# A compression weight tile in a spent chunk of the recurrence's table, and 32x32 products on two strips of columns

## The chip, the cores and the metric

The kernel runs on one core of one Trainium2 chip. The metric is the device time of one launch in microseconds (us); lower is better. The kernel before takes 841.3 us (median of 3 runs, 841.02 to 841.45).

## The reference, cut to what matters

One decoder block for 512 tokens of width 1024 in float32: a norm, one input projection (`w_in`), two mixers, gates, an output projection, and a gated MLP. The change touches the two mixers.

The attention mixer compresses its keys and values before it uses them: blocks of 32 tokens with stride 16 are flattened to 2048 numbers and go through a two-layer MLP with GELU.

```python
flat = blocks.transpose(0, 1, 3, 2, 4).reshape(b, n_cmp, g, CMP_BLOCK * dh)
return jax.nn.gelu(flat @ w1) @ w2          # w1: 2048 x 256, one for keys, one for values
```

The RWKV-7 mixer is a recurrence over tokens, for 8 heads of size 64:

```python
sa = jnp.einsum('bhij,bhj->bhi', state, a_t)
state = state * w_t[:, :, None, :] + sa[..., None] * b_t[:, :, None, :] + v_t[..., None] * k_t[:, :, None, :]
return state, jnp.einsum('bhij,bhj->bhi', state, r_t)
```

## The kernel before, in words

**Products.** Weights come in tiles of 512 KB. For most, ScalarE rounds the tile `raw` to `whi`, VectorE (sometimes GpSimd) makes the rest `wlo`, and TensorE multiplies the activations, likewise in two parts `hh` and `hl`, by both: 16 products with `whi`, 8 with `wlo` (`dense_fm_g`). A new tile is asked for by `wnext`: it issues the load of a tile further on (`wload`, L262 to L268), splits the next one (`wsplit_`), and hands out the one that is due. `raw` has three buffers (L266), `whi` and `wlo` two each. All these loads are issued by SyncE (SP), whose queue is in order: a load that waits holds up those behind it. The order of the loads is that of the generator `weight_tiles` (L215 to L256).

**Compression weights.** The first layer's weights come in four tiles for keys and four for values, (0,k), (0,v) to (3,k), (3,v), 512 rows each. They are used unsplit (`eng` is `None`), straight from `raw`, so a raw buffer is held until TensorE has read it. Between them stand gate tiles, called G1, G2, G3 and so on here: (0,k), (0,v), (1,k), (1,v), G1, (2,k), (2,v), G2, (3,k), (3,v), G3, G4, ...

**The recurrence** works on 8 chunks of 64 tokens. Its 64x64 tables for all chunks, head pairs and two halves are in `AB` (128 partitions x 8 chunks x 1024). Before the chunk loop, a lower triangle in each table is inverted. Its 32x32 diagonal blocks are inverted by VectorE (`Nn`, `Tn`, L618 to L633) and written back by transposes (L730, L735). The 32x32 block below the diagonal needs two products per table: `below` (L740) makes the first and puts it in `Y1`, `left` (L749) the second and puts it in `AB`. Each call does 16 tables for the two groups g (partitions 0 to 63 and 64 to 127) and evicts by ScalarE, one instruction per group:

```python
mm(ptr[g][half(g, 1), 32 * i:32 * i + 32], ABq[g][half(g, 0), q0 + i, 32:64], Y1[half(g, 0), q0 + i], ...)
act(Y1[half(g, 1), q0:q0 + 16].rearrange("p q s -> p (q s)"), ptr[g][half(g, 1)])
```

`half(g, b)` are partitions 64g + 32b to 64g + 32b + 31. TensorE's array is addressed by the partitions of the operands (strips of rows) and of the output (strips of columns). The inverse's block runs in TensorE's written order (L760 to L768): gate tile 0, `below(0)`, `below(16)`, a part of the key/value projection (`kv_proj`), `left(0)`, another part, `left(16)`, another part.

**The chunk loop** (L931 to L993), again in TensorE's written order, does for chunk c: products of the old state (`M`, `AR`), `Xs` copied out by VectorE, products `AB` x `Xs` and `AB` x `UV` of the next chunk, `UV` copied out by ScalarE (one half, L956) and VectorE (other half, L957), products of `UV` with `BKT` (new state) and with `AB` (output), and every second chunk a group norm on VectorE and ScalarE. Between these steps the generator `fill_chain` (L880) puts other TensorE work: the rest of the key/value projection, the compression (`compress`, L786), one pair of tiles at a time with 16 passes each, and gate tiles. The compression's input table `Rk` lies in `sg1` and is written by VectorE (L126, L790); it shares that memory with `Y1`. After pair 3 comes GELU on ScalarE and VectorE. ScalarE's and VectorE's own orders come from a scheduler.

**After the loop's chunk 3** the first half of `AB` is used again, for the bias rows `BT` (L907, loaded in chunks 4 and 5), and the second half for gates.

Of the kernel before, what the change touches and what calls it, by code (L numbers as in the profile page):

```python
# [10 lines left out]
F32 = mybir.dt.float32  # L11
# [69 lines left out]
def hybrid_block(ctx: ExitStack, tc: tile.TileContext, A: dict, out: bass.AP):  # L81
# [15 lines left out]
    wp = ctx.enter_context(tc.tile_pool(name="w", bufs=1))  # L97
# [12 lines left out]
    def mmb():  # L110
        return bank("mm", 4)

    def pa():
        return bank("a", 2)

    def pb():
        return bank("b", 2)

    def mm(o, l, r, start, stop):
        te.matmul(o, lhsT=l, rhs=r, start=start, stop=stop)  # L120

    def act(o, i, f=AF.Copy, **kw):
        sc.activation(o, i, f, **kw)  # L123
# [32 lines left out]
    for name in ("rwkv_mu", "rwkv_w0", "rwkv_a0", "rwkv_k_k", "rwkv_k_a", "rwkv_r_k", "rwkv_ln_g", "rwkv_ln_b"):  # L156
        r0, n = ROWS[name]
# [57 lines left out]
    def weight_tiles():  # L215
        def cols(w, o, kt=KT, eng=v):
            return w[:, o:o + 128], kt, 128, eng

        def rows(w, o, n, kt=KT, eng=v):
            step = 1024 // n  # L220
            for i, k0 in enumerate(range(0, kt, step)):
                kn = min(step, kt - k0)
                yield w[128 * k0:128 * (k0 + kn), o:o + n], kn, n, eng[i] if type(eng) is list else eng

        pool_ = nc.gpsimd
        yield cols(w_in, O_RWKV + 1536, eng=pool_)
        yield cols(w_in, O_RWKV + 1664, eng=pool_)
        for p in range(NH2):
            for o in (512, 0, 1024):
                yield cols(w_in, O_RWKV + o + 128 * p)  # L230
        yield cols(w_in, O_KC)
        yield from rows(w_in, O_Q, 512, eng=[v, pool_, ("spare", pool_), v])
        yield cols(w_in, O_VC)
        yield from rows(w_in, O_KS, 256, eng=[v, ("spare", v)])
        for m in range(NGA):
            yield cols(w_in, O_GA + 128 * m)
        yield from rows(w_in, O_KW, 280, eng=pool_)
        for m in range(NGA, KT):
            if m < 4:
                for s4 in range(m if m > NGA else 0, m + 1):  # L240
                    for s_ in "kv":
                        yield A["cmp_w1_" + s_][0][512 * s4:512 * s4 + 512], 4, 256, None
            yield cols(w_in, O_GA + 128 * m)
        for m in range(NGB):
            yield cols(w_in, O_GB + 128 * m)
        for m in range(KT):
            if m + NGB < KT:
                yield cols(w_in, O_GB + 128 * (m + NGB), eng=pool_ if m else v)
            yield cols(A["w_proj_b"][0], 128 * m, NH2, eng=pool_)
        for m in range(KT):  # L250
            yield cols(A["w_proj_a"][0], 128 * m, NH2)
        yield from rows(A["w_out"][0], 0, 512)
        yield from rows(A["w_out"][0], 512, 512, eng=())
        for f in range(NF):
            yield cols(A["w_up"][0], DFF + 128 * f)
            yield cols(A["w_up"][0], 128 * f)  # L256
        for hf in range(2):
            yield from rows(A["w_down"][0], 512 * hf, 512, NF)

    wtiles = weight_tiles()  # L260
    loads, ahead, late = [], [], []
    def wload():  # L262
        nxt = next(wtiles, None)
        if nxt is not None:
            src, kt, n, eng = nxt
            raw = wp.tile([128, kt, n], F32, name="raw", tag="raw", bufs=3)  # L266
            nc.sync.dma_start(raw, src.rearrange("(k p) n -> p k n", p=128))
            loads.append((raw, kt, n, eng))  # L268

# [29 lines left out]
    def wnext(kt, n):  # L299
        wload()  # L300
        if loads and loads[0][3] != ():
            wsplit()
        w = ahead.pop(0)
        assert list((w if type(w) is not tuple else w[0]).shape) == [128, kt, n]
        return w
# [3 lines left out]
    _, hs = norm_tiles(xp)  # L309
    ssx = xp.tile([128, NT], F32, name="ssx")  # L310
    wload()
    wload()
    wload()

# [16 lines left out]
    with tc.manual_schedule(engines={getattr(mybir.EngineType, e) for e in ("PE", "Activation", "DVE", "Pool")}):  # L331
# [20 lines left out]
        raw = loads.pop(0)[0]  # L352
# [73 lines left out]
    AB = abp.tile([128, NCH, NH2, 2, 128], F32, name="AB")  # L426
# [190 lines left out]
    ABq = [AB.rearrange("p c a r t -> p (c a) r t")[:, :, g, :] for g in range(2)]  # L617
# [4 lines left out]
    for g in range(2):  # L622
        for b in range(2):
            r = 64 * g + 32 * b
            v.transpose(Nn[r:r + 32].rearrange("p t s -> p t s"),
                        ABq[g][r:r + 32, :, 32 * b:32 * b + 32].rearrange("p q t -> p t q"))
    for k in range(31):
        m, n = 31 - k, k + 1
# [99 lines left out]
    Y1 = sg1[:, 1:3].rearrange("p m s -> p (m s)").rearrange("p (q s) -> p q s", q=32)  # L728
# [3 lines left out]
    for b in (1, 0):  # L732
        for g in range(2):
            r = 64 * g + 32 * b
            v.transpose(ABq[g][r:r + 32, :, 32 * b:32 * b + 32].rearrange("p q t -> p t q"), Tn[r:r + 32])  # L735

    def half(g, b):
        return slice(64 * g + 32 * b, 64 * g + 32 * b + 32)

    def below(q0):  # L740
        ptr = [pa(), pb()]
        for i in range(16):
            for g in range(2):
                mm(ptr[g][half(g, 1), 32 * i:32 * i + 32], ABq[g][half(g, 0), q0 + i, 32:64], Y1[half(g, 0), q0 + i],
                   True, True)
        for g in range(2):
            act(Y1[half(g, 1), q0:q0 + 16].rearrange("p q s -> p (q s)"), ptr[g][half(g, 1)])

    def left(q0):  # L749
        ptr = [pa(), pb()]  # L750
        for i in range(16):
            for g in range(2):
                mm(ptr[g][half(g, 0), 32 * i:32 * i + 32], Y1[half(g, 1), q0 + i], ABq[g][half(g, 1), q0 + i, 32:64],
                   True, True)
        for g in range(2):
            act(ABq[g][half(g, 0), q0:q0 + 16, 32:64], ptr[g][half(g, 0)].rearrange("p (q t) -> p q t", t=32))

    fill = kv_proj(1, 280)
    urgent.clear()
    with tc.manual_schedule(engines={mybir.EngineType.PE, mybir.EngineType.Pool}):  # L760
        for m in range(NGA):
            act(siga[m], dense_fm(hh, hl))
        below(0)
        below(16)
        next(fill)
        left(0)
        next(fill)
        left(16)  # L768
        next(fill)
        norm_keys(0)  # L770
        rstd(qss.rearrange("p t h -> p (t h)"), DH)
        for t in range(NT):
            nc.gpsimd.tensor_tensor(heads(qn[:, t]), heads(qn[:, t]), qss[:, t, :, None].to_broadcast([128, 8, DH]),
                                    op=ALU.mult)
# [505 lines left out]
    for i in range(KT // 2):  # L1280
        raw = loads.pop(0)[0]
# [9 lines left out]
    with tc.manual_schedule(engines=KTS):  # L1291
        for t in range(NT):
            qs = slice(128 * t, 128 * t + 128)
            p = mmb()
# [52 lines left out]
    for hf in range(2):  # L1347
        bo = dense_tok(512, aT[:, 0], aT[:, 1], NF)
        for t in range(NT):
            n = 256 if hf and t == NT - 1 else 512  # L1350
# [32 lines left out]
```

## Time and profile before

| | |
|---|---|
| median of 3 runs | 841.3 us (841.02 to 841.45) |
| profiled execution | 841.33 us |
| its span, first to last instruction | 839.5 us |
| TensorE products busy | 824.8 us, 98% |
| VectorE busy | 514.1 us, 61% |
| ScalarE busy | 405.4 us, 48% |
| GpSimd busy | 52.4 us, 6% |
| granted TensorE clock | 1.0 throughout |

All times in views are us from the start of the span. PE is TensorE (PEld its weight loads), DVE VectorE, ACT ScalarE, POOL GpSimd, SPq the issue of a DMA by SyncE. A row of a timeline is: start, length, engine, line of the kernel, operation, tile written <- tiles read, shape, count, and in brackets the engine's idle time before it with what ended it. The profile takes a float32 product as two passes, so 32 products show as x64. Nearly all products and evictions go through helpers, so they carry the lines L120 (product), L123 (ScalarE), L126 and L135 (VectorE); they are told apart by their tiles. `sg` stands for `sg0` and `sg1`, which `Y1` and `Rk` lie in, and `QK` for the buffer of GELU's operands among others.

### The profile page before, as it was taken

To read this page: it belongs to the slowest core of one execution; us is meant where nothing else is said; L and a number is where in the kernel's file an instruction comes from. 1 tells how busy PE (TensorE), PEld (TensorE's weight loads), DVE (VectorE), ACT (ScalarE), POOL (GpSimd) and SP (SyncE) were. 2 spreads that over 40 slices of the span, in tenths; PEclk is the share of its full clock that TensorE was granted. 3 is DMA by queue.
4 is the path that set the end of the run, shared out by engine and by line. 5 is a ranking of instruction groups with operands and counts; after the bars stand their busy time and mean duration, and the time that the engine had idled before them with its cause. 6 is when DMAs were issued, how large, how long until landed. Compare 5 with 4: busy or idle time off the path is not lost.

```text
span 839.5 us, 12845 instructions
## 1 busy us (share of the span) xinstructions
PE 824.8 (98%) x5097; PEld 669.9 (80%) x5097; DVE 514.1 (61%) x998; ACT 405.4 (48%) x784; POOL 52.4 (6%) x69
## 2 busy tenths in 40 slices
PE   7999999999999999999999999999999999999998
PEld 6777778887677876777788988888888888888886
DVE  5478779964556678888665566665555666322222
ACT  6766654452555767677343454444444444221210
POOL 5200020140000100111000000000000000000000
PEclk9999999999999999999999999999999999999999
DMA  7432222335462320000266033333333332233421
GB/s 229 113 80 72 76 76 77 83 102 168 128 126 62 84 57 13 26 26 26 63 222 206 1 101 100 94 90 93 101 101 101 100 96 89 92 101 113 138 75 51
DMA packets 109104, 78.73 MB, mean 94 GB/s; under 512 B 3869, under 2 KB 97748, under 8 KB 109044
## 3 DMA queue, kind: packets, MB, share of 16 engines
q1 hardware_dynamic: 106512, 73.51, 29.7%
q10 hardware_dynamic: 1060, 2.55, 1.0%
q0 software_dynamic: 1472, 1.86, 1.0%
q8 instruction: 40, 0.66, 0.3%
q14 instruction: 20, 0.16, 0.1%
HBM read 74.56 MB, written 2.29 MB: 92 GB/s over the span
## 4 chain that ended last, share of the span: by engine, by line
PE 53%; DVE 0%; DVEq 0%; issue 0%
PE ps_mm L120 52%; PE ps_b L203 0%; PE ps_a L203 0%; PE ps_a L120 0%; PE ps_b L1187 0%; PE ps_mm L1187 0%; DVE x L126 0%; DVEq L1379 0%; PE ps_a L1139 0%
## 5 line engine op out<-in xcount | busy, mean ns | idle before, releaser
L296 DVE TENSOR_TENSOR wlo<-raw,whi 128x1024 fp32r<-128x1024 f32 (+1 forms) x111 | 131.5, 1186 | 186.5 <-PE ps_mm L120 157.8
L120 PE MATMUL ps_mm<-hh,whi 128*128 128x512 f32 (+1 forms) x624 | 242.6, 391 | 0.7 <-ACT whi L123 0.7
L120 PE MATMUL ps_mm<-hl,whi 128*128 128x512 f32 (+1 forms) x624 | 240.4, 387 | 0.0
L123 ACT ACTIVATE whi<-raw 128x1024 fp32r<-128x1024 f32 (+3 forms) x124 | 123.3, 996 | 170.9 <-PE ps_mm L120 141.6
L120 PE MATMUL ps_mm<-hh,wlo 128*128 128x512 f32 (+1 forms) x624 | 151.7, 384 | 0.0
L120 PEld LDWEIGHTS ps_mm<-hh,whi 128*128 128x128 f32 x624 | 117.3, 188 | 27.5 <-ACT whi L123 1.1
L120 PEld LDWEIGHTS ps_mm<-hl,whi 128*128 128x128 f32 x624 | 117.4, 188 | 23.4 <-issue 1.0
L120 PEld LDWEIGHTS ps_mm<-hh,wlo 128*128 128x128 f32 x624 | 115.1, 188 | 23.3
L120 PE MATMUL ps_mm<-whi,aT 128*128 128x512 f32 x352 | 84.5, 390 | 0.0
L120 PEld LDWEIGHTS ps_mm<-whi,aT 128*128 128x128 f32 x352 | 65.9, 188 | 14.3 <-issue 0.4
L135 DVE SCALAR_TENSOR_TENSOR cgv<-ps_mm,cw,cgv 128x511 f32<-128x511 f32 (+1 forms) x88 | 65.4, 746 | 1.6
L123 ACT ACTIVATE cgv<-ps_mm,cw 128x512 f32<-128x512 f32 x44 | 34.3, 781 | 23.3 <-PE ps_mm L120 23.3
L120 PE MATMUL ps_mm<-wlo,aT 128*128 128x512 f32 x176 | 44.3, 389 | 0.0
L123 ACT ACTIVATE P<-P,nm 128x512 f32<-128x512 f32 (+3 forms) x64 | 35.4, 553 | 14.9 <-DVE nm L1161 14.9
L123 ACT ACTIVATE aT<-cgv 128x512 fp32r<-128x512 f32 x22 | 13.9, 632 | 56.8 <-DVE cgv L126 56.8
L120 PEld LDWEIGHTS ps_mm<-wlo,aT 128*128 128x128 f32 x176 | 33.0, 188 | 6.9
L123 ACT ACTIVATE cgv<-cgv 128x512 f32<-128x512 f32 x22 | 13.9, 632 | 41.0 <-DVE cgv L135 41.0
L296 POOL TENSOR_TENSOR wlo<-raw,whi 128x512 fp32r<-128x512 f32 (+3 forms) x13 | 20.4, 1569 | 204.3 <-PE ps_mm L120 148.5
L1161 DVE CUSTOM_DVE_ANT_0 P<-ps_a,AB 128x512 f32<-128x512 f32 (+3 forms) x64 | 29.4, 483 | 4.2 <-PE ps_a L120 3.7
L126 DVE TENSOR_TENSOR x<-x,ps_mm 128x512 f32<-128x512 f32 (+1 forms) x17 | 11.0, 654 | 23.0 <-PE ps_mm L120 21.2
L126 DVE TENSOR_TENSOR aT<-cgv,aT 128x512 fp32r<-128x512 f32 x22 | 15.2, 693 | 14.7 <-ACT aT L123 14.7
L120 PE MATMUL ps_a<-KH,qst 128*128 128x512 f32 (+3 forms) x64 | 21.3, 348 | 1.6 <-DVE nm L1161 0.9
(356 smaller groups left out, 1203.4 us busy)
## 6 DMA issues: line engine op xcount, KB each, us to landing
raw<-in_w_up_dram SPq DMA_DIRECT2D x44, 512.0 KB, 3.7
raw<-in_w_in_dram SPq DMA_DIRECT2D x38, 512.0 KB, 3.8
raw<-in_w_down_dram SPq DMA_DIRECT2D x22, 512.0 KB, 3.5
raw<-in_w_out_dram SPq DMA_DIRECT2D x8, 512.0 KB, 3.6
xt<-in_x_dram SPq DMA_DIRECT2D x4, 512.0 KB, 5.9
raw<-in_cmp_w_k_dram SPq DMA_DIRECT2D x4, 512.0 KB, 4.9
raw<-in_cmp_w_v_dram SPq DMA_DIRECT2D x4, 512.0 KB, 5.0
raw<-in_w_proj_b_dram SPq DMA_DIRECT2D x8, 256.0 KB, 2.7
```

Of the source, the lines that this page charges most:

```text
L120: te.matmul(o, lhsT=l, rhs=r, start=start, stop=stop)
L123: sc.activation(o, i, f, **kw)
L126: v.tensor_tensor(o, a, b, op=op)
L135: v.scalar_tensor_tensor(o, a, s, b, op0=op0, op1=op1)
L296: eng.tensor_tensor(lo, raw, hi.bitcast(F32), op=ALU.subtract)
L1161: v.tensor_tensor_reduce(out=P[:, i], in0=sp[:, N * (i - i0):N * (i - i0) + N], in1=BT[:, h, 384 - 128 * qt:512], scale=-1.0, scalar=-NEG, ...
```

## The change

Two edits.

1. The load of (3,k) doesn't go to one of the three raw buffers but to `AB[:, 0]`, chunk 0 of the recurrence's table, which has the same size. The tile is used from there. The raw buffer that it would have taken goes to a later tile.
2. In `below` and `left` the products of the tables alternate between the group's two strips of output partitions: even tables go to one, odd ones to the other. Each bank then holds 8 tables of 32 columns on each strip. The evictions become two per group, for the even and the odd tables, of 256 elements per partition instead of 512.

The order of TensorE's products is the same.

```diff
-                        yield A["cmp_w1_" + s_][0][512 * s4:512 * s4 + 512], 4, 256, None
+                        yield A["cmp_w1_" + s_][0][512 * s4:512 * s4 + 512], 4, 256, "ab" if (s4, s_) == (3, "k") else None
...
-            raw = wp.tile([128, kt, n], F32, name="raw", tag="raw", bufs=3)
+            if eng == "ab":
+                raw, eng = AB[:, 0].rearrange("p a r t -> p (a r t)").rearrange("p (k n) -> p k n", n=n), None
+            else:
+                raw = wp.tile([128, kt, n], F32, name="raw", tag="raw", bufs=3)
...
     def below(q0):
...
-                mm(ptr[g][half(g, 1), 32 * i:32 * i + 32], ABq[g][half(g, 0), q0 + i, 32:64], Y1[half(g, 0), q0 + i],
+                o = 32 * (i // 2)
+                mm(ptr[g][half(g, 1 - i % 2), o:o + 32], ABq[g][half(g, 0), q0 + i, 32:64], Y1[half(g, 0), q0 + i],
                    True, True)
         for g in range(2):
-            act(Y1[half(g, 1), q0:q0 + 16].rearrange("p q s -> p (q s)"), ptr[g][half(g, 1)])
+            for e in range(2):
+                act(Y1[half(g, 1), q0 + e:q0 + 16:2],
+                    ptr[g][half(g, 1 - e), 0:256].rearrange("p (q s) -> p q s", s=32))
...
     def left(q0):
...
-                mm(ptr[g][half(g, 0), 32 * i:32 * i + 32], Y1[half(g, 1), q0 + i], ABq[g][half(g, 1), q0 + i, 32:64],
+                o = 32 * (i // 2)
+                mm(ptr[g][half(g, i % 2), o:o + 32], Y1[half(g, 1), q0 + i], ABq[g][half(g, 1), q0 + i, 32:64],
                    True, True)
         for g in range(2):
-            act(ABq[g][half(g, 0), q0:q0 + 16, 32:64], ptr[g][half(g, 0)].rearrange("p (q t) -> p q t", t=32))
+            for e in range(2):
+                act(ABq[g][half(g, 0), q0 + e:q0 + 16:2, 32:64],
+                    ptr[g][half(g, e), 0:256].rearrange("p (q t) -> p q t", t=32))
```

## Prediction

> **What bounds the kernel now.** I read the page first. TensorE is busy 98% of the span, so time is won only where TensorE gets less to do or waits less.
>
> ```profile
> span 839.5 us, 12845 instructions
> ...
> PE 824.8 (98%) x5097; PEld 669.9 (80%) x5097; DVE 514.1 (61%) x998; ACT 405.4 (48%) x784; POOL 52.4 (6%) x69
> ```
>
> Next the view of waits for TensorE over the whole span. Behind the wait for the first constants stand three that belong together: the copy `UV` on VectorE, the splitting `whi` on ScalarE, and `UV` on ScalarE.
>
> ```profile
> PE ps_a L120 <- DVE UV L957: 1.1, 1, 1.1
> ...
> PE ps_mm L120 <- ACT whi L123: 0.7, 1, 0.7
> ...
> PE ps_a L120 <- ACT UV L123: 0.2, 1, 0.2
> ```
>
> The timeline of 202.5 to 222.4 us shows where they lie: in chunk 2 of the recurrence, round the last pair of compression tiles. I call these (3,k) and (3,v), and the gate tiles split between them G2, G3, G4.
>
> ```profile
> 202.61 0.37 SPq L267 DMA_DIRECT2D raw<-in_cmp_w_k_dram  x1
> 203.48 0.37 SPq L267 DMA_DIRECT2D raw<-in_cmp_w_v_dram  x1
> 203.94 18.26 SPq L267 DMA_DIRECT2D raw<-in_w_in_dram  x6
> ...
> 209.50 2.16 PE L120 MATMUL ps_mm<-raw,sg 128*64 128x256 f32 x16
> 211.25 1.06 ACT L123 ACTIVATE whi<-raw 128x1024 fp32r<-128x1024 f32 x1 [4.42 <-DMA raw<-in_w_in_dram]
> ...
> 212.34 1.23 DVE L296 TENSOR_TENSOR wlo<-raw,whi 128x1024 fp32r<-128x1024 f32 x1 [3.86 <-ACT whi L123]
> 212.36 0.50 PE L120 MATMUL ps_mm<-hh,whi 128*128 128x512 f32 x1 [0.69 <-ACT whi L123]
> ...
> 214.07 0.41 DVE L946 COPY Xs<-ps_b 128x256 f32<-128x256 f32 x1
> ...
> 214.41 0.16 DVE L132 TENSOR_SCALAR rs_m<-n 128x8 f32<-128x8 f32 x1
> ...
> 215.30 0.27 PE L120 MATMUL ps_b<-Xs,AB 64*64 64x64 f32 x2
> ...
> 216.70 0.68 DVE L126 TENSOR_TENSOR Ys<-Ys,n 128x512 f32<-128x512 f32 x1
> ...
> 217.30 0.41 DVE L126 TENSOR_TENSOR QK<-QK,ps_mm 128x256 f32<-128x256 f32 x1
> 217.44 1.06 ACT L123 ACTIVATE whi<-raw 128x1024 fp32r<-128x1024 f32 x1 [3.19 <-DMA raw<-in_w_in_dram]
> ...
> 218.71 0.36 ACT L123 ACTIVATE UV<-ps_b 64x256 f32<-64x256 f32 x1
> 219.12 0.33 PE L120 MATMUL ps_a<-UV,BKT 128*64 128x64 f32 x2 [0.18 <-ACT UV L123]
> ...
> 220.12 0.43 DVE L957 COPY UV<-ps_b 64x256 f32<-64x256 f32 x1
> ...
> 220.60 0.62 PE L120 MATMUL ps_a<-UV,BKT 128*64 128x64 f32 x13 [1.15 <-DVE UV L957]
> ...
> 221.68 0.50 PE L120 MATMUL ps_mm<-hh,whi 128*128 128x512 f32 x1
> ```
>
> Three loads leave SP one behind the other, (3,k), (3,v), G3. G3, third in line, is split at 211.25, the moment it lands, and TensorE stands 0.69 us for it. G4 gets its buffer only after that, lands at about 217.4, and its split stands in ScalarE's and VectorE's streams ahead of both halves of `UV`, which the recurrence needs. TensorE came to the products of `UV` at 218.94 (the row of 219.12 less its 0.18 of idle time), made two, stood another 1.15 us and went on at 220.60. The 16 compression products from 209.50 add 0.2 us:
>
> ```profile
> 200.02 1.95 PE L120 MATMUL ps_mm<-raw,sg 128*64 128x256 f32 x16
> 201.90 0.50 PE L120 MATMUL ps_mm<-hh,whi 128*128 128x512 f32 x1
> ```
>
> They took 1.95 us one pair earlier, and 2.16 here, as (3,v) was landing. In all 0.2 + 0.69 + 0.18 + 1.15 = 2.2 us are lost in this stretch.
>
> **The load.** (3,k) gets a place of its own, chunk 0 of `AB`, and one of the three raw buffers is free for what follows. In the built order of the changed kernel its load stands in SP's queue right behind G1's and ahead of (2,k), (2,v) and G2. It waits for the last reader of chunk 0 and for the evictions of the inverse, long done. Behind it wait those three loads, and TensorE waits for them from 200.02 on.
>
> ```profile
> 190.54 0.64 PE L120 MATMUL ps_a<-UV,AB 128*64 128x64 f32 x16
> ```
> ```profile
> 193.16 0.37 SPq L267 DMA_DIRECT2D raw<-in_cmp_w_k_dram  x1
> ```
>
> The last reader is the first row, done at 191.2. (2,k) is issued at 193.16 at the earliest, since it takes G1's buffer and G1 is split until then. The added wait ends 2 us earlier and costs nothing; without that cover it would delay (2,k) by its excess. The bias rows, which overwrite chunk 0, are loaded in chunks 4 and 5, long after (3,k) is read in chunk 2: nothing there either.
>
> The three slots at 202.61, 203.48 and 203.94 now carry (3,v), G3 and G4, on the same conditions (G2 split, pair 2 read). I let them land as the three land now: the third at 211.2, the second at about 209.7 (where pair 3 stopped stretching). Then, in times of the trace before:
> - Pair 3 runs 209.50 to 211.38. G3 is split from 209.75, ready at 210.8: TensorE's 0.69 us go.
> - The 12 products after it take 2.94 us (212.36 to 215.30) and end at 214.32. But in the built order G4's split now stands on ScalarE and VectorE ahead of the group norm's square and of `Xs`. It falls where G3's stands now (211.25, 212.34), so `Xs` ends at 214.48 as it does now, and the `Xs` products start at 214.55 instead of 215.30: 0.75 us won.
> - From there TensorE needs 3.64 us to the `UV` products (215.30 to 218.94): 218.19. VectorE has, before `UV`, eleven small steps of the group norm, one each 0.2 us from 214.41 (`Ys` follows the eleventh at 216.70 now), GELU's three (1.0 in all, the one of 217.30 being among the longer) and `Ys` (0.6): 218.2 + 0.43 = 218.65 against 220.55 now. No split is among them any more.
>
> The block starts at 218.65 instead of 220.60: **2.0 us** won of 2.2. The bounds are 0.75 (the first step alone stays) and 2.2. I take 2.0, since it follows from rows of these same instructions.
>
> **The strips.** The windows view counts TensorE's products in the four blocks of the inverse, in `below` (both halves) and twice in `left`. Two more rows show 64x64 products, first on two parts of the array (`UV` alone), then on four (`Xs` and `UV`). The columns are window, length, busy time (count), clock.
>
> ```profile
> 168.93:171.08 2.15, 2.15 (x129) 1.00 0.04 8
> 174.37:175.50 1.13, 1.13 (x65) 1.00 0.02 5
> 177.23:178.36 1.13, 1.13 (x65) 1.00 0.00 0
> 180.49:181.11 0.62, 0.62 (x18) 1.00 0.06 16
> 187.25:187.89 0.64, 0.64 (x34) 1.00 1.08 384
> ```
>
> The blocks take 4.41 us for 256 passes on two parts of the array. With 64x64, twice the parts did twice the passes (32 for 16) in the same time. The changed products go to four parts, two strips of rows by two of columns, as `Xs` and `UV` do. By these rows half of what lies above some 0.1 us of start in each block goes: 1.0 + 0.5 + 0.5 = 2.0 us. The bounds are 0 (issue or weight loads forbid it) and 2.0; the 64x64 rows are the nearest, so I take 2.0.
>
> Not all of it stays. VectorE (third busy time of the first row, windows view of all engines) works without a gap until the compression table is written:
>
> ```profile
> 170.00:180.00 10.00, 10.00 (x250) 9.57 (x243) 9.92 (x28) 5.69 (x10) 3.16 (x3) 1.00 0.18 57
> ```
> ```profile
> 180.50 1.28 DVE L126 TENSOR_TENSOR sg<-QK,prm 128x248 f32<-128x248 f32 x2
> ```
> ```profile
> 183.25 1.95 PE L120 MATMUL ps_mm<-raw,sg 128*64 128x256 f32 x16
> ```
>
> The table is ready at 181.78, whatever TensorE does, and the products that read it start at 183.25 now. TensorE would come at 181.25 and stand until about 181.85. **1.4 us** remain.
>
> One rule speaks against the strips. In the Trainium skill, the page "TensorE: Matmul & The Clock Gate", part 3 "Packing small matmuls", says that a weight load overlaps a running product only when it goes to another strip of rows. The two strips of one group g share their rows, so by it this part would give 0 and the sum 839.3. The windows of the products of `cw2` (128 rows each, first one strip of columns, then four) speak against it: 8 in 0.47 us, then the other 16 within 0.24 (its count also holds three still running).
>
> ```profile
> 237.93:238.40 0.47, 0.47 (x8) 1.00 1.22 124
> 238.40:238.64 0.24, 0.24 (x19) 1.00 1.05 98
> ```
>
> The evictions double in number and halve in size:
>
> ```profile
> 170.33 0.59 ACT L123 ACTIVATE sg<-ps_a 32x512 f32<-32x512 f32 x1
> ...
> 172.17 0.59 ACT L123 ACTIVATE sg<-ps_b 32x512 f32<-32x512 f32 x1
> ```
> ```profile
> 206.06 0.77 ACT L123 ACTIVATE Ys<-ps_a 64x256 f32<-64x256 f32 x2 [3.32 <-PE ps_a L120]
> ```
>
> Eight at 0.385 (the 256-element row) end at 173.4, not 172.76. The first `left` needs the first four (171.9) and would start at 173.35; the second needs the last and comes at 175.7. The second `left`'s four end at about 177.8, and its reader comes at 178.5. So they cost 0; without cover at most 0.64 us for `below` and 0.3 for each `left`.
>
> **Sum.** The profiled execution took 841.33 us (span 839.5 and 1.8 around it), the median is 841.3, so the two are one number here. 841.33 - 1.4 - 2.0 = **837.9 us**. From 222 us on TensorE is dense, and its loads follow its own progress, so the gain should last.
>
> **The rivals.**
> - *The strips don't overlap* (issue, or the rule above). Against it the four-part rows. 841.3 - 2.0 = 839.3. Chance 0.15.
> - *The wait for `UV` stays*: VectorE's GELU and group norm, which stand ahead of it, turn out as late as the splits did. For it: the built order leaves `UV` last of that chain. Only 0.75 us of the load's gain stays: 841.3 - 1.4 - 0.75 = 839.2. Chance 0.15.
> - *G4 becomes the recurrence's gate* (the slower side). Its split now stands ahead of `Xs` in two in-order streams, so each us that G4 lands after 211.2 delays the recurrence by one. From 214.6 on the whole change loses. Were it to land when it does now, 217.4, `Xs` would end 6.2 us later than forecast and the `Xs` products start at 220.75, 5.45 after today's: 841.3 + 5.45 - 1.4 = 845.4. Against it: its slot on SP is the one in which G3 lands by 211.2. Chance 0.07.
> - *Nothing happens*: (3,k) arrives earlier but the stretch is bound by the transfers, and strips don't overlap: 841.3. Chance 0.08.
>
> **How the numbers follow.** The forecast has 0.55. Its own spread is 837.1 (2.2 from the load and all 2.0 of the strips) to 838.8 (1.5 and 1.0). The two cases at 839.2 and 839.3 belong in the range: 837.0 to 840.0, leaving out some 0.15 to 0.2. A difference under 0.2% (1.7 us) can't be told from none, so 839.6 is the border. Faster: 0.55 and three quarters of the two partial cases, 0.77; within 0.2%: the rest of those and the last rival, 0.16; slower 0.07.
>
> **What would show it.** In the profile of the changed kernel: `below` lasting about 1.15 us and each `left` 0.6 with the same counts; pair 0 of the compression starting near 181.85 behind VectorE; (3,k) issued at about 190 and (2,k) not later than 192; no wait of TensorE for `whi` in chunk 2 and at most 0.6 us for `UV`; evictions near 0.37 us. The forecast is wrong if the strips' blocks keep their length, if `Xs` of chunk 2 ends well after 213.1 (214.5 less the strips' 1.4), or if a load behind (3,k) slips.

## The result, and the profile after

The changed kernel takes 837.83 us (median of 6 runs, 837.64 to 838.38) against 841.33 (median of 6, 841.02 to 842.76): a ratio of 0.9959, 95% interval 0.9948 to 0.9969. The profiled execution took 837.9 us; its span is 836.1 us, 3.4 less than before.

From the page of the changed kernel, the span and TensorE's row:

```profile
span 836.1 us, 12860 instructions
...
PE 822.2 (98%) x5097; PEld 667.1 (80%) x5097; DVE 514.2 (62%) x998; ACT 406.7 (49%) x792; POOL 52.4 (6%) x69
```

TensorE is as full as it was, with as many products; 2.6 us of its busy time are gone. From its waits over the whole span:

```profile
PE ps_b L337 <- DMA kc<-in_consts_dram: 5.1, 1, 5.1
...
PE ps_mm L120 <- ACT whi L123: 0.5, 1, 0.5
```

The two waits for `UV` (1.1 and 0.2) are no longer in the list. The wait for `whi` is, with 0.5 instead of 0.7, but it is another one, as the next rows show.

**The blocks of 32x32 products**, windows of TensorE's products in the changed kernel (window, length, busy time and count, clock, DMA share, GB/s), `below` and twice `left`:

```profile
168.87:170.14 1.27, 1.27 (x129) 1.00 0.00 0
173.43:174.12 0.69, 0.69 (x66) 1.00 1.08 384
175.85:176.54 0.69, 0.69 (x66) 1.00 0.00 0
```

2.65 us for the passes that took 4.41. The evictions, two of 256 elements in 0.76 to 0.78 us, hold nothing. The last of `below` end at 173.40, and the first `left` starts at 173.43:

```profile
172.62 0.78 ACT L123 ACTIVATE sg<-ps_b 32x256 f32<-32x256 f32 x2
```

**Pair 0 of the compression**, timeline of the changed kernel round it, VectorE's last writes of the table and TensorE:

```profile
180.69 1.27 DVE L126 TENSOR_TENSOR sg<-QK,prm 128x248 f32<-128x248 f32 x2
...
181.40 2.56 PE L120 MATMUL ps_mm<-raw,sg 128*64 128x256 f32 x16
183.88 0.40 PE L120 MATMUL ps_mm<-whi,hh 128*128 128x280 f32 x1
```

The 16 passes take 2.56 us and not 1.95: the first reads the keys' table, which is done, and the next ones wait for the values' table, done at 181.96. The view of waits doesn't list this; only the length of the group tells it.

**G2**, timeline of the changed kernel, loads, the split, and TensorE:

```profile
190.01 0.37 SPq L270 DMA_DIRECT2D AB<-in_cmp_w_k_dram  x1
191.58 0.37 SPq L270 DMA_DIRECT2D raw<-in_cmp_w_k_dram  x1
192.08 0.42 SPq L270 DMA_DIRECT2D raw<-in_cmp_w_v_dram  x1
192.62 0.43 SPq L270 DMA_DIRECT2D raw<-in_w_in_dram  x1
```
```profile
198.77 1.95 PE L120 MATMUL ps_mm<-raw,sg 128*64 128x256 f32 x16
201.24 0.50 PE L120 MATMUL ps_mm<-hh,whi 128*128 128x512 f32 x1 [0.52 <-ACT whi L123]
```
```profile
200.13 1.06 ACT L123 ACTIVATE whi<-raw 128x1024 fp32r<-128x1024 f32 x1 [8.09 <-DMA raw<-in_w_in_dram]
```

(3,k) leaves first, then (2,k), (2,v) and G2. G2's load is issued 1.6 us earlier than before (194.21), but G2 is split, as it lands, only 0.1 us earlier (200.13 against 200.26 in the profile before). TensorE comes 1.2 us earlier and stands 0.52 us. That is the wait for `whi` in the list.

DMA's view gives the time from the issue of a load to its landing (last number, us). For G2 it is, in the kernel before, in the changed kernel, and in the last run below, in which (3,k) is held back until it leaves behind G2:

```profile
raw<-in_w_in_dram SPq DMA_DIRECT2D x1, 512.0 KB, 6.0
raw<-in_w_in_dram SPq DMA_DIRECT2D x1, 512.0 KB, 7.4
raw<-in_w_in_dram SPq DMA_DIRECT2D x1, 512.0 KB, 6.6
```

So G2 takes 1.4 us longer in the changed kernel. Its end there is a long tail: for half a microsecond 0.07 of the 16 DMA engines are busy, about one. Windows of the changed kernel, then of the kernel before, round the end of G2's transfer (columns as above):

```profile
198.50:199.00 0.50, 0.50 (x26) 1.00 0.25 65
199.00:199.50 0.50, 0.50 (x8) 1.00 0.07 20
```
```profile
199.00:199.50 0.50, 0.50 (x7) 1.00 0.97 243
199.50:200.00 0.50, 0.50 (x32) 1.00 0.12 29
```

**Chunk 2**, timeline of the changed kernel, ScalarE's two splits (G3, G4), VectorE's copies, and TensorE:

```profile
208.21 1.06 ACT L123 ACTIVATE whi<-raw 128x1024 fp32r<-128x1024 f32 x1 [2.04 <-DMA raw<-in_w_in_dram]
209.92 1.06 ACT L123 ACTIVATE whi<-raw 128x1024 fp32r<-128x1024 f32 x1 [0.66 <-DMA raw<-in_w_in_dram]
```
```profile
212.75 0.41 DVE L956 COPY Xs<-ps_b 128x256 f32<-128x256 f32 x1
...
215.91 0.69 DVE L126 TENSOR_TENSOR Ys<-Ys,n 128x512 f32<-128x512 f32 x1
216.63 0.43 DVE L967 COPY UV<-ps_b 64x256 f32<-64x256 f32 x1
```
```profile
210.73 0.50 PE L120 MATMUL ps_mm<-hh,whi 128*128 128x512 f32 x1
...
217.25 0.69 PE L120 MATMUL ps_a<-UV,BKT 128*64 128x64 f32 x16
...
218.33 0.50 PE L120 MATMUL ps_mm<-hh,whi 128*128 128x512 f32 x1
```

No wait is left here. G4 is split before the rest of the group norm, `UV` is copied from 216.63 to 217.06, and TensorE, which nothing held since 210.73, comes to the products of `UV` 0.2 us after that copy ends.

TensorE's order is the same in both kernels, so the lead of the changed one (time of an instruction before, less its time now) shows where time was won and lost:

| place | before | after | lead |
|---|---|---|---|
| end of the three blocks | 4.41 us long | 2.65 us long | 1.76 |
| pair 0 begins | 183.25 | 181.40 | 1.85 |
| pair 0 ends (begin and length) | 185.20 | 183.96 | 1.24 |
| pair 2 begins | 200.02 | 198.77 | 1.25 |
| gate product of G2 | 201.90 | 201.24 | 0.66 |
| gate product of G3 | 212.36 | 210.73 | 1.63 |
| gate product behind the `UV` products | 221.68 | 218.33 | 3.35 |

After that nothing changes: the spans differ by 3.4.

### The profile page after: what moved, and what is told of

Read it like the earlier page. It is cut to its first block, busy times and chain, and to the rows that moved or that the text cites. A ratio compares the mean times of both kernels' runs of the same rounds, so it can differ in the third digit from the quotient of the medians.

```text
span 836.1 us, 12860 instructions
## 1 busy us (share of the span) xinstructions
PE 822.2 (98%) x5097; PEld 667.1 (80%) x5097; DVE 514.2 (62%) x998; ACT 406.7 (49%) x792; POOL 52.4 (6%) x69
## 4 chain that ended last, share of the span: by engine, by line
PE 53%; DVE 0%; DVEq 0%; issue 0%
PE ps_mm L120 52%; PE ps_a L203 0%; PE ps_b L203 0%; PE ps_a L120 0%; PE ps_b L1197 0%; PE ps_mm L1197 0%; DVE x L126 0%; DVEq L1389 0%; PE ps_a L1149 0%
```

## The experiments

Times are medians; a ratio is against the kernel before in runs on the same chip.

| run | us | ratio (95% interval) |
|---|---|---|
| load edit alone | 839.38 | 0.9975 (0.9965 to 0.9984) |
| strips alone | 839.15 | 0.9974 (0.9964 to 0.9984) |
| (2,k) in `AB` instead of (3,k) | 838.16 | 0.9964 (0.9952 to 0.9976) |
| table ahead of the norms | 837.69, again 837.29 | 0.9955 (0.9943 to 0.9968), 0.9953 (0.9940 to 0.9965) |
| before, 8 products twice | 841.08 | 0.9993 (0.9985 to 1.0002) |
| four strips | 837.68 | 0.9952 (0.9940 to 0.9965) |
| (2,k), G4's rest on GpSimd | 838.80 | 0.9970 (0.9958 to 0.9981) |
| chunk 1 instead of chunk 0 | 837.52 | 0.9951 (0.9937 to 0.9964) |
| load of (3,k) held | 844.97 | 1.0041 (1.0028 to 1.0054) |
| the same, one element moved | 838.32 | 0.9963 (0.9950 to 0.9977) |
| changed kernel again | 838.13 | 0.9960 (0.9947 to 0.9974) |

**Each edit alone.** The first takes the diff's part 1 only, the second its part 2 only.

> The load edit alone; the 32x32 products stay on one strip per group. Theory: in the changed kernel the load edit is worth 2.7 us in chunk 2 (no wait for the split of G3, none for UV) and costs about 0.6 us one stretch earlier, because four tiles, (3,k), (2,k), (2,v) and G2, are now in flight together, so that G2 lands late. That cost belongs to the load edit, so alone it gives 841.3 - 2.7 + 0.6 = 839.2 us, with a wait of TensorE for whi of 0.4 to 0.8 us near 202 us. Rival: G2 is late only because the strips bring TensorE to it 1.2 us earlier; then the load edit alone has no such wait and gives 838.6. Rival: the wait for UV goes only with both edits; 840.6 (the first 0.7 us alone).

> The strips alone; (3,k) goes to a raw buffer as before. Theory: the three blocks of 32x32 products get 1.7 us shorter, 0.5 us of it is given back at pair 0 of the compression, which waits for its table from VectorE, and 1.2 us stay; the stall of 2.2 us in chunk 2 stays as it was, 1.2 us earlier: 840.1 us, with waits of about 1.1 us for UV and 0.7 for whi. Rival: that stall is set by the transfers and not by TensorE's own progress; then the strips' gain disappears in it and the time is 841.3.

839.38 and 839.15, that is 2.1 and 2.3 us less than before (841.49). The load edit alone came as the theory had it, with a wait for G2 that is smaller than expected:

```profile
PE ps_mm L120 <- ACT whi L123: 0.2, 1, 0.2
```

The strips alone won 1 us more than the theory. Waits of the run with the strips alone, TensorE, 100 to 230 us:

```profile
PE ps_a L120 <- DVE UV L967: 1.1, 1, 1.1
...
PE ps_a L120 <- ACT UV L123: 0.2, 1, 0.2
```

`UV` is waited for as before, but the wait for G3's split is gone, although its load stands where it stood. The timeline of that run shows its load's issue and its split:

```profile
202.96 0.45 SPq L270 DMA_DIRECT2D raw<-in_w_in_dram  x1
```
```profile
208.86 1.06 ACT L123 ACTIVATE whi<-raw 128x1024 fp32r<-128x1024 f32 x1 [3.26 <-DMA raw<-in_w_in_dram]
```

5.9 us from issue to split; before it was 7.3 (203.94 to 211.25). So about 1 us of what the load edit wins is also won by the strips, and can be won only once: 2.1 + 2.3 less 1.0 is 3.4, the two together gave 3.5. The rest of the load edit's gain, at `UV`, comes with that edit alone: the run without it keeps these waits.

**Why G3 came late.** In DMA's view of the kernel before, 204 to 206 us, two packets of instructions lie among the first of the three loads (queue, packets, MB, share of 16 engines):

```profile
q8 instruction: 1, 0.02, 3.1%
q14 instruction: 1, 0.01, 1.0%
```

In the run with the strips alone the larger one came between 201 and 203 us. If that is the cause, TensorE's instructions need only be shifted. The kernel before, with nothing of the change:

```diff
-                mm(ptr[g][half(g, 0), 32 * i:32 * i + 32], Y1[half(g, 1), q0 + i], ...)
+                for _ in range(2 if q0 + 16 * g + i < 8 else 1):
+                    mm(ptr[g][half(g, 0), 32 * i:32 * i + 32], Y1[half(g, 1), q0 + i], ...)
```

> The kernel before with nothing of the change, but the first 8 products of the first `left` are issued twice (same operands, same output), which gives TensorE 32 more instructions ahead of the chunk loop and some 0.27 us more work (16 passes at 17 ns). Question: why did the wait for the split of G3 (0.7 us, with the slow pair 3 about 1.0) go in the kernel with the strips alone, where the loads stand as before? Theory: in the kernel before two fetches of instructions (16 KB and 8 KB, at 205.46 and 205.52) fall among the three loads and the last piece of each lands 2.1 us behind the first; where the 16 KB fetch falls earlier (201 to 204 us) the lag is 0.2 to 0.8. 32 instructions bring TensorE's fetch some 2 to 3 us earlier, so the wait goes: 841.4 + 0.3 - 1.0 = 840.7 us. Rival: the wait goes through what the strips do to the orders of the engines; then it stays here and the time is 841.7.

The 16 KB packet moved to 201 to 203 us (DMA's view of this run in that window), ahead of the loads, which were issued 1 us later than before:

```profile
q8 instruction: 1, 0.02, 3.4%
```
```profile
205.00 0.45 SPq L267 DMA_DIRECT2D raw<-in_w_in_dram  x1
```
```profile
211.07 1.06 ACT L123 ACTIVATE whi<-raw 128x1024 fp32r<-128x1024 f32 x1 [3.46 <-DMA raw<-in_w_in_dram]
```
```profile
210.29 1.95 PE L120 MATMUL ps_mm<-raw,sg 128*64 128x256 f32 x16
212.18 0.50 PE L120 MATMUL ps_mm<-hh,whi 128*128 128x512 f32 x1
```

6.1 us from issue to split, pair 3 in 1.95 us, no wait for G3. TensorE does more work and is still 0.2 us ahead of the kernel before at that product (212.36). The median is 0.55 us lower, 0.4 above what was expected (840.7) and 0.6 below the rival (841.7); the interval just takes in 1, so it is the trace that decides. That the wait goes when TensorE's instructions are shifted is shown, by this one shift. That the packets hold up one of the 16 DMA engines is a reading that fits, not shown: which engine carried them the trace doesn't tell. The load edit alone fits as well: there the 16 KB packet came at 203 to 205 us, as the loads began, and the third of them, G4's, was split after 6.9 us (204.44 to 211.30), in the changed kernel, with no packet there, after 6.3.

**The order of the loads.** One word differs: (2,k), which is needed first, goes to `AB`.

```diff
-... 4, 256, "ab" if (s4, s_) == (3, "k") else None
+... 4, 256, "ab" if (s4, s_) == (2, "k") else None
```

> The changed kernel, but the tile that goes to chunk 0 of AB is (2,k) and not (3,k). Its load leaves at the same moment, and then (2,v), G2 and (3,k) follow in the order in which they are needed: the tile in AB no longer stands ahead of tiles that are needed before it. Theory: G2 lands about 1.7 us earlier (one transfer less ahead of it), so the wait of 0.5 us for its split goes and the 0.6 us are won: 837.2 us. Rival: the late landing of G2 is not the extra transfer but its own issue; then 837.8. On the other side: G4 now takes a buffer that is freed only by the split of G3, lands near 213.6 instead of 209.8 and is split ahead of UV; if that holds UV, 838.3 or more.

838.16: not won. G2 lands earlier and isn't waited for, as expected (its split begins at 198.61), but then `UV` is. Waits of TensorE and VectorE's timeline in this run:

```profile
PE ps_a L120 <- DVE UV L967: 0.3, 1, 0.3
```
```profile
213.86 1.23 DVE L299 TENSOR_TENSOR wlo<-raw,whi 128x1024 fp32r<-128x1024 f32 x1 [0.41 <-ACT whi L123]
...
217.06 0.43 DVE L967 COPY UV<-ps_b 64x256 f32<-64x256 f32 x1
```

G4 got its buffer late, and its rest `wlo` stands in the middle of the group norm. This is the side expected as a loss: it cost what the other won.

**The table.** VectorE's order in the inverse's block is written out, and the compression's first step is taken there.

```diff
-    with tc.manual_schedule(engines={mybir.EngineType.PE, mybir.EngineType.Pool}):
+    with tc.manual_schedule(engines={mybir.EngineType.PE, mybir.EngineType.Pool, mybir.EngineType.DVE}):
...
         next(fill)
+        cp_ = compress()
+        next(cp_)
         norm_keys(0)
```

> The changed kernel, with VectorE's order written out in the inverse's block so that the table of the compression comes right behind the transposes, ahead of the norms of q and k. Theory: in the changed kernel pair 0 takes 2.5 instead of 1.95 us since its second table is finished by VectorE at 182.0; with the table done by 179.6 pair 0 takes 1.95 us and starts when TensorE comes to it, 0.55 us are won and the strips' whole 1.7 us stay: 837.3 us. Rival: the stretch of pair 0 comes from the landing of its weights or of the second layer's weights; then 837.8. Rival: the wait for G2 takes up what is won; 837.8 with a wait for whi of about 1.0 us.

Pair 0 has its old length (timeline of this run, TensorE, and VectorE's last part of the table):

```profile
181.34 1.95 PE L120 MATMUL ps_mm<-raw,sg 128*64 128x256 f32 x16
```
```profile
178.14 1.66 DVE L126 TENSOR_TENSOR sg<-QK,prm 128x248 f32<-128x248 f32 x3
```

The table is done at 179.8. So it was the table that stretched pair 0, and not its weights. In the time little of it is seen, so the run was repeated beside the changed kernel.

> The changed kernel with VectorE's table ahead of the norms once more, on the same chip: by its trace 0.65 us are won at pair 0 and 0.1 to 0.2 of it is kept from being lost again at G2, so 837.3 us; by its first five runs 837.7. If it comes out at 837.6 or above, the gain at pair 0 is taken back by the wait for G2.

> The changed kernel once more, on the chip of the run with the held load, so that the two can be compared: 837.8 us.

837.29 beside 838.13, and 837.69 beside 837.83 earlier; spans of the profiled executions 835.2 and 835.3 against 836.1 and 836.5. By the traces this version is 0.8 to 1.3 us faster than the changed kernel, by the medians 0.1 and 0.8 (the first profiled execution, 837.04, was the fastest of its five); the intervals of the ratios overlap. It is the best version here, by about as much as can be told.

**Four strips**, on top of that version; tables i % 4 to the four strips, four evictions of 128 elements per group.

```diff
-                o = 32 * (i // 2)
-                mm(ptr[g][half(g, 1 - i % 2), o:o + 32], ...)
+                o, e = 32 * (i // 4), 32 * (i % 4)
+                mm(ptr[g][e:e + 32, o:o + 32], ...)
```

> The changed kernel with VectorE's order of the run before (table ahead of the norms), and the 32x32 products on four strips of columns per group instead of two; the evictions become four per group of 128 elements. Theory that strips still double the rate: the 256 passes, 4.4 us on one strip and 2.7 on two, take about 1.9 on four; 837.7 - 0.8 = 836.9 us, less what ScalarE's 32 evictions hold back. Rival: at two strips the passes already follow each other at 8.8 ns, near what the sequencer can issue; then the blocks keep their 2.7 us and the time is 837.7, or more if the evictions (some 4.5 us for the 16 behind `below`) hold the first `left`: 838.2.

837.68, the time of two strips. Windows of `below` and the first `left` in this run:

```profile
168.79:170.06 1.27, 1.27 (x130) 1.00 0.00 0
173.34:174.03 0.69, 0.69 (x66) 1.00 1.07 381
```

To the hundredth as with two. `left` has 64 passes fewer than `below` and takes 0.58 us less: 9.1 ns for a pass, with two strips and with four, against 15.9 with one ((2.15 - 1.13) / 64). The rival holds: past two strips something else limits the passes.

**G4's rest on GpSimd**, with (2,k) in `AB` and the table ahead:

```diff
-            yield cols(w_in, O_GA + 128 * m)
+            yield cols(w_in, O_GA + 128 * m, eng=pool_ if m == 4 else v)
```

> Meant to beat the rest: strips, VectorE's table ahead of the norms, (2,k) instead of (3,k) in chunk 0 of AB, and the rest wlo of G4 made by GpSimd instead of VectorE, so that no split stands ahead of UV in VectorE's stream. Theory: in the trace with (2,k) the wait for G2 (0.4 to 0.6 us) had gone and a hold of 0.6 us at UV had come, because VectorE made the rest of G4 ahead of UV's copy; with that on GpSimd both are gone: 837.7 - 0.45 = 837.2 us, no wait of TensorE in chunks 1 and 2. Rival: UV is held by the group norm and GELU steps of VectorE and not by the split; then the hold of some 0.6 us stays and the time is 837.8.

838.80, worse than either. GpSimd's, then VectorE's timeline of this run, and for comparison the same step of VectorE in the changed kernel:

```profile
213.79 2.39 POOL L299 TENSOR_TENSOR wlo<-raw,whi 128x1024 fp32r<-128x1024 f32 x1 [18.27 <-DVE rs_y L135]
```
```profile
214.01 2.32 DVE L132 TENSOR_SCALAR QK<-QK 128x256 f32<-128x256 f32 x1 [0.30 <-ACT QK L123]
...
217.82 0.43 DVE L968 COPY UV<-ps_b 64x256 f32<-64x256 f32 x1
```
```profile
213.97 0.29 DVE L132 TENSOR_SCALAR QK<-QK 128x256 f32<-128x256 f32 x1
```

A step of 0.29 us takes 2.32 and ends 0.15 us after GpSimd's. The split didn't leave VectorE's stream; it became a stall in it, and GELU's step on ScalarE, which needs its result, held ScalarE's half of `UV` too (1.4 us of wait there).

**A place that comes free later.** `AB[:, 0]` replaced by `AB[:, 1]`.

> The changed kernel, but (3,k) goes to chunk 1 of AB, which the recurrence gives up one chunk later (about 205.6 instead of 190.0 us). It tests the slower side: a place that comes free too late. SP takes this load behind G2, and (3,v), G3 and G4 wait behind it. Theory: no wait for G2 (0.6 us won), but the loads that left at 202.5 to 203.6 leave at 205.7 to 206.8, so pair 3 waits for (3,v) until about 211 instead of 209.1, and G3 and G4 land some 2 to 3 us later: 837.8 - 0.6 + 2.0 + about 1 = 840.2 us, and up to 842 if the split of G4 holds UV again. Rival: the freed raw buffer makes up for the late place; then 837.8 or less.

This run doesn't test what it was meant to. The load is issued in the program ahead of the chunk's last reads, so it doesn't wait for them: it left at 198.71, and chunk 1 of the recurrence worked on the weights that lay there. What it computes is no longer the block. Its time shows a load order alone, (3,k) behind G2: 837.52, with 0.3 us of wait for G2. There G2 took 6.2 us from issue to landing, but was issued 0.8 us later than in the changed kernel (193.43), so the wait has another cause than there. What a place that comes free too late would cost stays open.

**(3,k) held back**, with the table ahead; in `wload`, ahead of the load to `AB`:

```diff
+                nc.gpsimd.tensor_tensor(hold, ahead[0][0:1, 0, 0:1], AB[0:1, 0, 0, 0, 0:1], op=ALU.add)
```

`hold` is a tile of one element in the pool of constants.

> Meant to beat the rest: the kernel with VectorE's table ahead of the norms (strips, (3,k) in chunk 0 of AB), and the load of (3,k) held back until (2,k) has landed: a one-element sum of GpSimd reads (2,k) and chunk 0, and the load waits for it, so it stands behind G2 in SP's queue and leaves near 195.5 instead of 189.4 us. Theory: what made G2 late was the transfer of (3,k) ahead of it; now G2 lands about 1 us earlier, the wait for its split (0.4 us in the run without the hold) goes, and nothing else changes, since (3,k) is needed only at 208: 837.7 - 0.4 = 837.3 us, against the changed kernel some 0.5 less. Rival: G2 is late through its own issue and the fetches; then 837.7 with that wait still there. Rival: (3,k) now delays (3,v), G3 and G4; then a wait for UV or whi in chunk 2 and 838 or more.

844.97, 3.6 us slower than before. The waits don't show why: the one for G2 is gone, `UV` is waited for 0.6 us, and at 222 us TensorE led the kernel before by 3.6 us. It then lost 6.6 us between 490 and 740 us, evenly and without a wait (the expectation below says 7.5, which was read too high). The next run has the same hold, but the one element lies in the recurrence's own pool.

> The run with the held load came out at 845.0 us: its TensorE was 3.6 us ahead of the kernel before at 222 us and lost 7.5 us evenly between 490 and 740 us, where 38 products of the MLP took 8.87 instead of 8.61 us. Its only other difference is a tile of one element among the constants, which moves most tiles by 32 bytes (the activations' high part from 22368 to 22400). Here the one element lies in the recurrence's own pool, and those tiles keep their places; the hold of the load is the same. Theory: the 7.5 us came from the places of the tiles; then 844.97 - 7.4 = 837.6 us, with 38 products in 8.61 us. Rival: they came from the held load or the GpSimd instruction; then 845. As for the hold itself: no wait for G2, but a hold of about 0.6 us at UV, which VectorE's stream sets, so no gain over 837.3 to 837.7.

838.32. Windows of TensorE's products from 500 to 700 us, first the run with `hold` among the constants, then this one (the count is what matters; the kernel before has 884 too):

```profile
500.00:700.00 200.00, 200.00 (x859) 1.00 0.32 94
```
```profile
500.00:700.00 200.00, 200.00 (x884) 1.00 0.33 96
```

Full both times, at the same clock, but 3% fewer products. The place of the tiles did it. As for the hold, it took the wait for G2 away, and `UV` took its place, 0.7 us here:

```profile
PE ps_a L120 <- DVE UV L970: 0.7, 1, 0.7
```

In these two runs a part of the group norm stands in VectorE's stream between the splits of G3 and G4 and not ahead of both, so its stream to `UV` ends later. G2 didn't land faster by the hold: 6.7 and 6.6 us from its issue, against 6.6 and 6.5 with the table ahead and no hold. The expectation that the transfer of (3,k) is what makes G2 late isn't borne out.

## Why the prediction was right

837.9 was predicted, 837.8 came. The main mechanisms held: the strips overlap, and the waits in chunk 2 go. That the sum fits to 0.1 us is partly luck, as its pieces were less exact than that; and the changed kernel took 838.1 when it was run again.

- *Strips, 2.0 raw, 1.4 kept.* Right in kind; 1.76 raw and 1.24 kept. The rate didn't quite double: 9.1 ns per pass where half of 15.9 is 8. The cap was where the prediction put it, VectorE's table, and gave back 0.61 us (1.85 to 1.24) for the 0.6 foreseen. It did so otherwise than foreseen: pair 0 starts at 181.40 and not near 181.85, and is stretched. The run with the table ahead shows that it was the table. The rule of the Trainium skill that was weighed ("TensorE: Matmul & The Clock Gate", part 3 "Packing small matmuls") would have had the blocks keep 4.41 us; they took 2.65 with the same rows in each group, so the trace speaks against it here.
- *Evictions, nothing.* Right: 0.38 us each, no wait in their place.
- *The load, 2.0.* 2.1 net, but of other pieces: +0.97 at G3, +1.72 at `UV`, -0.59 at G2.
- *The step that failed: the added load "costs nothing".* The prediction looked at the wait of SP's queue, which indeed cost nothing, since (2,k) left 1.6 us earlier, and not at the transfers. G2 was asked for 1.6 us earlier, took 1.4 us longer to land, and 0.59 us were lost there. With the load edit alone the wait is there too (0.2), and with (2,k) in the place it is gone. Why G2 is late stays open. From issue to landing it took 6.5 to 7.4 us in the six runs with (3,k) ahead of it, and 6.0 to 6.2 in the four in which G2 is third and nothing was moved ahead. But it took 6.6 and 6.7 in the two with the hold, where G2 is third too. In those two and in the six, packets of instructions fell among these loads (in the changed kernel at 193 to 195 and 197 to 199 us), and in the four none did while their data moved. With (2,k) in the place G2 is third of four, such packets are there, and it took 6.3 and 6.1. So neither the fourth load nor the packets alone explain it, and no run parts the two.
- *The wait for G3, put down to the place in the queue.* Too narrow. It goes with the strips alone, and with 8 doubled products and no other change. So the place in the queue wasn't what made it; a shift of the instructions ended it. The prediction charged it to the load edit, with the right sum only because it is won once.
- *The wait for `UV`.* Right in kind: G4's split no longer stands late in VectorE's stream, and the copy ends at 217.06, for a forecast of 218.65 less the strips' 1.4, 217.25. That the products of `UV` start at 217.25 to the hundredth is luck: TensorE came there by its own stream, 0.2 us after the copy. So G2's delay cost little in the end. Had TensorE come 0.6 us earlier, with VectorE's stream as it is, it would have stood for the copy, and all but some 0.2 us would have been lost again (an estimate from these rows).
- *Rivals.* Strips that don't overlap and a wait for `UV` that stays: both ruled out by the rows. G4 as the gate: not here, since `Xs` is copied by 213.16 and its products start at 213.68. With (2,k) in the place G4 is split 2.9 us later (212.77), and `UV` is waited for 0.3 us. The 1.4 us with GpSimd come from VectorE's stall.

What the wait for G2 alone is worth stays open: each run that took it away also moved G4 or VectorE's order.

## What to carry to other kernels

When a load gets a place of its own and starts early, look not only at the queue it is issued from but at when the tiles behind it land: G2, asked for earlier, came no earlier here. Giving the place to the next tile due took that wait away, and made a later tile late instead. Two edits that each win 2 us may both be winning the same microsecond; run each alone before their gains are added. Where TensorE waits for an in-order engine, ask what stands in that engine's stream ahead of the awaited instruction: taking one wait away can bring the next, `UV` for G2, and work given to GpSimd can stall VectorE for as long as it runs.

## What the runs showed of the hardware

- Passes of 32x32 on one strip follow each other at 15.9 ns, on two at 9.1, on four at 9.1.
- VectorE stood for the length of an instruction of GpSimd's: a step of 0.29 us took 2.32 beside GpSimd's 2.39. The Trainium skill's page "SBUF — State Buffer", section "SBUF: two separate sides", says that the two share a pair of ports under an exclusive lock and that the loser blocks fully; these rows agree.
- A tile of one element among the constants, which moves most tiles (by 32 bytes, as the expectation above has it), made TensorE's products in the MLP 3% slower (859 against 884 in 200 us) at the same granted clock and with no wait. Which tile's place matters wasn't tried.
- Of three loads of 512 KB in a row the third was split 5.9 to 6.3 us after its issue (G2 and G3 in the runs above in which no load was added ahead of them), and 7.3 where two packets of instructions fell among them within 0.1 us.
